# Eleven operations moved within the order of a hybrid attention/RWKV block, and one small product given to VectorE

## The chip, the cores and the metric

The kernel runs on one core of a Trainium2 chip. The metric is the device time of one execution in microseconds. A core has five instruction queues that matter here: TensorE (PE in the profile, its weight loads PEld), VectorE (DVE), ScalarE (ACT), GpSimd (POOL) and SyncE (SP), which issues the DMAs. Each engine works through its own queue strictly in order; between engines there are only semaphores.

## What is computed

The reference is one decoder block for a sequence of 512 positions and a model width of 1024: an RMS norm, one input projection, then two groups of heads side by side (native sparse attention, "NSA", and the RWKV-7 recurrence), one output projection and a gated ConvFFN. Everything is float32. Cut to what matters:

```
h = rmsnorm(x, norm1_g);  proj = h @ w_in
# attention: 8 heads, 2 groups; compressed, selected and window branch, each with its gate
o_nsa  = gates0 * softmax(q k_cmp + bias) v_cmp + gates1 * softmax(q k_sel + bias) v_sel + gates2 * softmax(q k_win + bias) v_win
# RWKV-7: 8 heads, state 64x64, 512 steps
sa = state . a
state = state * w + sa x b + v x k
y = state . r                       # then a norm over the head, + bonus, * gate g
x = x + concat(o_nsa, o_rwkv) @ w_out
h = rmsnorm(x, norm2_g);  u = causal_dwconv(h @ ffn_up)
x = x + (silu(u_gate) * u_val) @ ffn_down
```

## The kernel before

**Products.** Matrix products keep float32 accuracy by splitting each operand into a high and a low part (ACT casts `hi<-raw`, DVE or POOL subtracts `lo<-raw,hi`) and adding three products. Weights stream from DRAM through a ring of tiles.

**Stages.** `prep(j)`, j = 0 to 3, prepares two RWKV heads: the decay `sgw` (an ACT tanh, a DVE TENSOR_SCALAR, a DVE scan along time), its exponentials `W` and `iW` on ACT, the normalised key `kkn`, then `Af`, `AR`, `BK`, `BKh` (scaled copies for the chunks), `rl` (low part of the bonus product) and `Ma`, `Mr` (masked 64x64 products, from PSUM tile `rp`). `inverse(g)` inverts triangular 32x32 blocks for a pair of `prep`s: `Z <- Z,U` product and `Z <- Z` sum, 31 times. `chain(g)` then runs 16 chunk steps: in `step(c)` TensorE multiplies the state, DVE adds `UV <- rw,AV`, TensorE multiplies `UV` by `BKt`, and DVE adds `Sb <- sw,rw` (state times decay `sw <- Sb,wcs`, plus the new part); each pair of chunks gives an output `py`, normed by `norm` into `yn`. In parallel, attention has `queries` (`qd <- qs,rq`, a product by the query norm), `scores` (softmax numerators `L`, statistics `st`), `values` (`ph` cast by ACT, `pl` subtracted by DVE, then TensorE adds `ot <- ph,Vt` and `ot <- pl,Vt`) and `merge` (`of`). Output projection and ConvFFN follow, from about 370 us to the end.

**What sets the order.** The program text does not. Engines are wrapped (`_Eng`, lines 199 to 213): every call is put on a list and numbered, and `_Order.release` (line 190) issues the list at the end in the order of the table `TURNS` (line 174, 5,996 numbers, packed in the string `_TURNS`). So all instructions have line 210 in the profile and are told apart by tile names. `SWAP` (line 177) holds numbers of `tensor_tensor` calls that go to the other one of VectorE and GpSimd than their text says. Which buffer of a ring a tile takes, and so what it must wait for, follows from the same order.

```
    def release(self, turns):
        ...
            for i in turns:
                self.held[i]()
```
```
            swap = name == "tensor_tensor" and self._o.held is not None and len(self._o.held) in SWAP
            f = getattr(self._x if swap else self._e, name)
```

Of the kernel before, what the change touches and what calls it, by code (L numbers as in the profile page):

```python
# [32 lines left out]
_o = 0  # L33
for _n, _w in (("ident", 128), ("mask", 128), ("reset", 512), ("sel", 2), ("ones", 1), ("row", 1)):
# [83 lines left out]
    "j~{QtBV{oSxFCh--RAzvS~C!!K;{3P&y%0*+oJlJuk}&hw)uG(wlDm1}wpKjLeIdhwm-SI<x+m;{qNI8Keku>LVMfeFr&1jOsnAPZt}*`$oP99%Mof-izE"
    "gS33^S-GX>%)DTKkRf7Uuz|fe6u8#ng1BJkU)cRnJ`48nd>}ZXF~N2-4BO0~X@N0V7i>1${>HLkt8u&(bVE11hOV9kK^Hto_lGdgd}!vI4|x7iKj2jt^kM"
    "12!7$J8U?|V+F_di&;kW)g4}E~)!3h37!3+yV`I7NEJQx%V4m#_r+6#jMM@#t^&jWe%(6;(caE9adm3GtaS_Nf1<q*v=e+nhhJNQf=q#BBo8v1GwtIcSQo"  # L120
    "q`aVutEP|vnM6Wqo%*#EJ(-MnipBfDq405UPnqE&fg5kB$=g>)(kR<v#b34C7&<nW``q51Elxl^5llKhPD-&X_m7h73S-EI{X2~=vd8$F*;I5Yxdx}T$j6"
    "&HOLyI(RjHkgLDw@CrE;%4c<kdjvT=yfgYlfrwOtIGajSi2B-9A>LdeKggy2W?I)4*ah?5{v+Syz*3+6o8?mOd|4X#zW1Lk-aY8R>ZEDl4E;aR}e6I(kuI"
    "9i7nPrd3DcvJ`<ft6saZG<ShdFc3>0J5JY?LjsRc6U<Jtc0%SR*lJi$22@Yqe~o-uFn1uIDq3`BB(L*2;ceu4~M8%@x-AQgcHW%M#h4C&)I=m-i^o_hb{9"
    "YgXwht`S=`LL+sxE;7)mW~#qCQR20}UC26a+*av2_UMudCP=(gm&>ekg;()%Q8%(qtY5?WOMe+5qvQ?gCtK9%V+ns<tUY9moFcEAlj7(lCrA(J#`3duln&"
    "J{5|a0bgqWy~Ov##<<$QJ{w%AkNX1!%v4Bc6?C+~EX&RSEt$Ua@5D|8uku~--B%hFdvd_+FhKIHzL8uF(8nVG1p<zxn?p|;eM9$H80N=><KvKn_aS{<28R"
# [1157 lines left out]
```

## Time and profile before

| | us |
|---|---|
| three runs | 799.33, 792.83, 798.37 (median 798.37) |
| the profiled execution | 796.21, its span in the trace 794.3 |
| busy in that span: PE / DVE / ACT / POOL | 766.3 / 517.5 / 359.6 / 227.0 |
| mean granted TensorE clock | 0.984 of full |

The span is what the profiler recorded, from the first instruction to the last; 1.9 us of the profiled execution lie around it. Busy time is the time in which at least one instruction of the engine was running. In a row of the timeline, the part in square brackets is the engine's idle time just before the row and what ended it: `[1.94 <-DVE kkn L210]` is 1.94 us of idling that ended when DVE had written `kkn`.

### The profile page before, as it was taken

The page shows a single profiled execution, that of the slowest core. Times are in us where ns is not written, and L with a number is a line of the kernel's source. Part 1 is how long each engine was busy: PE and PEld are TensorE (multiplying, and loading weights), DVE is VectorE, ACT ScalarE, POOL GpSimd, SP SyncE. Part 2 cuts the span into 40 slices and gives each one's busy share as a digit, 9 for nine tenths or more (in the row PEclk, how much of TensorE's full clock was granted, in tenths as well). Part 3 has the DMA queues.
Part 4 walks back from the last instruction along what each step waited for, and adds up shares of the span by engine and source line. Part 5 has one row for each costly group of instructions (what it writes and reads, how often), then busy time and mean ns, then how long its engine had stood idle before and what let it go on. Part 6 is the DMA issues. An engine that isn't in the chain of part 4 may idle for free.

```text
span 794.3 us, 12056 instructions
## 1 busy us (share of the span) xinstructions
PE 766.3 (96%) x4152; PEld 617.0 (78%) x4152; DVE 517.5 (65%) x1078; ACT 359.6 (45%) x779; POOL 227.0 (29%) x360
## 2 busy tenths in 40 slices
...
DMA packets 59708, 67.87 MB, mean 85 GB/s; under 512 B 25710, under 2 KB 32686, under 8 KB 59648
## 3 DMA queue, kind: packets, MB, share of 16 engines
...
## 4 chain that ended last, share of the span: by engine, by line
PE 86%; DVE 7%; POOL 3%; issue 2%; ACT 1%; DMA 1%; SPq 0%; DVEq 0%; POOLq 0%; ACTq 0%
PE mm L210 31%; PE rp L210 23%; PE rw L210 21%; PE ot L210 5%; PE pre L210 4%; PE py L210 2%; POOL Z L210 1%; DVE Z L210 1%; DVE sgw L210 1%; DMA raw<-in_wst 1%; DVE Sb L210 0%; DVE sw L210 0%; DVE Ma L210 0%; DVE UV L210 0%; DVE qd L210 0%
## 5 line engine op out<-in xcount | busy, mean ns | idle before, releaser
L210 ACT CAST hi<-raw 128x512 fp32r<-128x512 f32 (+3 forms) x212 | 117.4, 584 | 127.2 <-DMA raw<-in_fdn 67.2
L210 DVE TENSOR_TENSOR lo<-raw,hi 128x512 fp32r<-128x512 f32 (+3 forms) x179 | 118.3, 672 | 39.8 <-ACT hi L210 15.4
L210 DVE SCALAR_TENSOR_TENSOR uf<-zf,fvt,uf 128x512 f32<-128x512 f32 x88 | 65.7, 749 | 29.4 <-ACT uf L210 29.4
L210 ACT ACTIVATE uf<-zf,fvt 128x512 f32<-128x512 f32 x44 | 35.8, 816 | 98.4 <-DVE zf L210 98.4
L210 POOL MEMSET zf<- 128x2 f32 x44 | 4.2, 100 | 211.3 <-DVE uf L210 107.5
L210 POOL TENSOR_TENSOR lo<-raw,hi 128x512 fp32r<-128x512 f32 (+3 forms) x33 | 39.8, 1210 | 68.3 <-ACT hi L210 28.8
L210 PE MATMUL mm<-act,hi 128*128 128x512 f32 x176 | 55.2, 395 | 0.0
L210 PE MATMUL mm<-h2h,hi 128*128 128x512 f32 x128 | 50.7, 396 | 0.0
L210 PE MATMUL mm<-h2l,hi 128*128 128x512 f32 x128 | 50.5, 395 | 0.0
L210 PE MATMUL mm<-h2h,lo 128*128 128x512 f32 x128 | 50.5, 394 | 0.0
L210 PE MATMUL rw<-h2h,hi 128*128 128x512 f32 x112 | 44.3, 395 | 0.0
L210 PE MATMUL rp<-h2l,hi 128*128 128x512 f32 x112 | 44.2, 394 | 0.0
L210 PE MATMUL rw<-h2l,hi 128*128 128x512 f32 x112 | 44.2, 394 | 0.0
L210 PE MATMUL rp<-h2h,hi 128*128 128x512 f32 x112 | 44.1, 396 | 0.0
L210 PE MATMUL rp<-h2h,lo 128*128 128x512 f32 x112 | 44.1, 394 | 0.0
L210 PE MATMUL rw<-h2h,lo 128*128 128x512 f32 x112 | 44.1, 394 | 0.0
L210 POOL TENSOR_TENSOR L<-L,st 128x512 f32<-128x512 f32 (+1 forms) x41 | 38.9, 968 | 5.7 <-PE rw L210 2.3
L210 ACT ACTIVATE L<-L,st 128x384 f32<-128x384 f32 (+3 forms) x64 | 35.4, 557 | 8.2 <-DVE st L210 5.4
L210 PEld LDWEIGHTS mm<-act,hi 128*128 128x128 f32 x176 | 33.0, 188 | 7.8
L210 PE MATMUL mm<-K,Q 128*128 128x256 f32 (+3 forms) x128 | 34.0, 362 | 2.8 <-DVE pl L210 2.1
L210 PE MATMUL mm<-act,lo 128*128 128x512 f32 x88 | 34.7, 394 | 0.0
L210 PE MATMUL mm<-XH,hi 128*128 128x512 f32 x80 | 32.8, 412 | 0.7 <-ACT hi L210 0.7
...
## 6 DMA issues: line engine op xcount, KB each, us to landing
...
```

Source lines behind the costliest of these rows:

```text
L210: self._o.held.append(lambda: f(*a, **k))
```

## The change

The packed table `_TURNS` is replaced by another of the same length, so that eleven operations stand elsewhere in the order, and one number leaves `SWAP`. A line or two of the diff:

```
-    "c-rlncbHX0(#GFDBRQubgCdHAAqR&jARuYUk|c;IK|ojmMOkuO$r(gI6v;V9k+>>?7#M<p$bbxjBbi~QtG>7UUKDkC_WAy2e$P4g+;hA8R99DbRrMJIgOU"
+    "c-rlncX(CB*2dr2k=~?*4hkyLA}wI(Ris_IpeQJUbi_+hkV|h~dXXkg6a`UwM*)MtRS`smP^3vHK`_z@$*lFgGv^?vm*+m;|K#`VefHUBX7<dQHLJ{yfkE"
...
-SWAP = {..., 2321, 2322, 2364, 2366, ...}
+SWAP = {..., 2321, 2322, 2366, ...}
```

The new file is one line shorter, so every row of it says L209. What the table moves, by place in the program (the numbers are those of the places in the text below):

1. GpSimd, the second pair of `prep`s: `XT` (a memset of a buffer that the inverse fills much later) and `AR` exchange their places around `rl`.
2. VectorE, a step of `chain(0)`: one of the two `sw <- Sb,wcs` goes up by four operations.
3. VectorE, a step later: `UV` goes ahead of `yn <- yn,py`.
4. VectorE: one `qd <- qs,rq` (128x4x64, half of a query product) goes down past `UV`, `sw`, `yb` and two `Sb`.
5. VectorE, a few steps later: `UV` goes ahead of one `Z <- Z` and of the reciprocal `zc`.
6. `st <- st,gates` (128x4) of one `scores` goes from GpSimd to VectorE, between a `CUSTOM_DVE`/accumulator read of `L` and the product `L <- L,st` that uses it.
7. VectorE, at the end of the inverse of the second pair: `pl <- rp,ph` goes ahead of the last `Z <- Z,U`, the last `Z <- Z` and a `TENSOR_SCALAR st`.
8. ScalarE, late in `chain(1)`: the first of two `yn <- py` goes behind `COPY of` and `CAST ph`.

TensorE's and SyncE's orders are the same in both.

Place 1, GpSimd's queue in the second pair of `prep`s; before:

```order
L210 TENSOR_TENSOR BKh<-BK,W 128x512
L210 MEMSET XT 128x1024
L210 TENSOR_TENSOR rl<-KR,rh 128x512
L210 TENSOR_TENSOR AR<-KR,W 128x16x32
L210 TENSOR_TENSOR lo<-raw,hi 128x512
```

and now:

```order
L209 TENSOR_TENSOR BKh<-BK,W 128x512
L209 TENSOR_TENSOR AR<-KR,W 128x16x32
L209 TENSOR_TENSOR rl<-KR,rh 128x512
L209 MEMSET XT 128x1024
L209 TENSOR_TENSOR lo<-raw,hi 128x512
```

`AR` needs the exponential `W` from ACT, `rl` and `XT` need nothing from it; `BKh` ahead of them and `lo` behind them stand where they stood.

Place 2, VectorE's queue around a step of the first chain (`z`, `VV` belong to the projection, `rq` is the query norm, `bs` a row of biases); before:

```order
L210 TENSOR_TENSOR UV<-rw,AV 32x256
L210 COPY bs<-mm 8x512
L210 SCALAR_TENSOR_TENSOR VV<-z,omm,zp 128x16x32
L210 TENSOR_TENSOR Sb<-sw,rw 64x2x64
L210 TENSOR_TENSOR yb<-yb,v_613 128x256
L210 TENSOR_TENSOR Ma<-rp,cct 128x256
L210 TENSOR_SCALAR rq<-rq 128x4x8
L210 TENSOR_TENSOR sw<-Sb,wcs 64x128
L210 TENSOR_TENSOR Sb<-sw,rw 64x2x64
```

and now:

```order
L209 TENSOR_TENSOR UV<-rw,AV 32x256
L209 COPY bs<-mm 8x512
L209 TENSOR_TENSOR sw<-Sb,wcs 64x128
L209 SCALAR_TENSOR_TENSOR VV<-z,omm,zp 128x16x32
L209 TENSOR_TENSOR Sb<-sw,rw 64x2x64
L209 TENSOR_TENSOR yb<-yb,v_613 128x256
L209 TENSOR_TENSOR Ma<-rp,cct 128x256
L209 TENSOR_SCALAR rq<-rq 128x4x8
L209 TENSOR_TENSOR Sb<-sw,rw 64x2x64
```

`sw` went from just ahead of the `Sb` that adds it to a place ahead of `VV`; behind that second `Sb` the order goes on with `Mr`, `Ma` and a `qd <- qs,rq` as before.

Places 3 and 4, VectorE's queue some three steps later (`m_629` and `yb` are the norm of `py`, `Q_582` and `Q_587` the low parts of queries); before:

```order
L210 TENSOR_TENSOR yn<-yn,py 128x256
L210 TENSOR_TENSOR UV<-rw,AV 32x256
L210 TENSOR_TENSOR sw<-Sb,wcs 64x128
L210 TENSOR_TENSOR Sb<-sw,rw 64x2x64 x2
L210 SCALAR_TENSOR_TENSOR Q_582<-rp,fvt,Q_582 64x2x256
L210 TENSOR_TENSOR qd<-qs,rq 128x4x64
L210 TENSOR_REDUCE m_629<-py 128x4
L210 TENSOR_TENSOR UV<-rw,AV 32x256
L210 TENSOR_TENSOR sw<-Sb,wcs 64x128
L210 TENSOR_SCALAR m_629<-m_629 128x4
L210 TENSOR_TENSOR yb<-py,m_629 128x256
L210 TENSOR_TENSOR Sb<-sw,rw 64x2x64 x2
```

and now:

```order
L209 TENSOR_TENSOR UV<-rw,AV 32x256
L209 TENSOR_TENSOR yn<-yn,py 128x256
L209 TENSOR_TENSOR sw<-Sb,wcs 64x128
L209 TENSOR_TENSOR Sb<-sw,rw 64x2x64 x2
L209 SCALAR_TENSOR_TENSOR Q_582<-rp,fvt,Q_582 64x2x256
L209 TENSOR_REDUCE m_629<-py 128x4
L209 TENSOR_TENSOR UV<-rw,AV 32x256
L209 TENSOR_TENSOR sw<-Sb,wcs 64x128
L209 TENSOR_SCALAR m_629<-m_629 128x4
L209 TENSOR_TENSOR yb<-py,m_629 128x256
L209 TENSOR_TENSOR Sb<-sw,rw 64x2x64 x2
L209 TENSOR_TENSOR qd<-qs,rq 128x4x64
```

`UV` and `yn` have exchanged their places at the top, and `qd` stands four operations and two `Sb` lower, ahead of `Q_587` instead of `m_629`.

## Rows read from the trace of the kernel before

**Rows 1.** Windows: stretch, length, busy time (instructions) PE, PEld, DVE, ACT, POOL, granted clock, DMA.

```profile
385.00:790.00 405.00, 405.00 (x1750) 327.21 (x1749) 225.58 (x344) 152.97 (x253) 23.82 (x60) 1.00 0.30 97
111.00:114.00 3.00, 3.00 (x15) 2.17 (x15) 2.17 (x5) 1.68 (x3) 1.23 (x1) 0.50 0.36 98
213.60:220.00 6.40, 6.38 (x27) 4.25 (x28) 5.26 (x12) 0.46 (x1) 1.85 (x3) 0.50 0.00 0
241.00:275.00 34.00, 29.01 (x258) 22.98 (x259) 30.70 (x107) 20.46 (x70) 27.84 (x61) 1.00 0.12 28
```

**Rows 2.** Timeline around place 1: start, duration (us), engine, operation, out<-in, [idle before].

```profile
103.87 1.31 DVE L210 TENSOR_SCALAR sgw<-sgw 128x512 f32<-128x512 f32 x1
...
104.87 1.46 POOL L210 TENSOR_TENSOR rl<-KR,rh 128x512 fp32r<-128x512 f32 x1
...
105.22 2.20 DVE L210 TENSOR_TENSOR_SCAN sgw<-cct,sgw 128x512 f32<-128x512 f32 x1
...
109.41 1.70 DVE L210 SCALAR_TENSOR_TENSOR Af<-kkn,W 128x512 f32<-128x512 f32 x1
...
109.53 0.30 PE L210 MATMUL rp<-cct,BKh 128*128 128x128 f32 x1 [1.94 <-DVE kkn L210]
```

**Rows 3.** Timeline of the decay of another `prep`, VectorE.

```profile
153.57 0.42 DVE L210 TENSOR_SCALAR sgw<-sgw 128x512 f32<-128x512 f32 x1
...
156.82 1.22 DVE L210 TENSOR_TENSOR_SCAN sgw<-cct,sgw 128x512 f32<-128x512 f32 x1
```

**Rows 4.** Timeline around place 2.

```profile
208.32 0.75 DVE L210 SCALAR_TENSOR_TENSOR VV<-z,omm,zp 128x512 f32<-128x512 f32 x1 [1.69 <-ACT zp L210]
...
210.42 2.73 DVE L210 TENSOR_TENSOR sw<-Sb,wcs 64x128 f32<-64x128 f32 x1
210.67 2.33 POOL L210 TENSOR_TENSOR qd<-qs,rq 128x256 f32<-128x256 f32 x4
...
213.61 0.40 POOL L210 TENSOR_TENSOR sw<-Sb,wcs 64x128 f32<-64x128 f32 x1 [0.62 <-DVE Sb L210]
213.62 0.61 PE L210 MATMUL rw<-Sb,AR 128*32 128x128 f32 x2 [3.88 <-DVE Sb L210]
...
214.09 1.06 POOL L210 TENSOR_TENSOR BKh<-BK,W 128x512 f32<-128x512 f32 x1
...
214.17 1.26 DVE L210 TENSOR_TENSOR qd<-qs,rq 128x256 f32<-128x256 f32 x1
...
215.80 0.42 DVE L210 TENSOR_TENSOR UV<-rw,AV 32x256 f32<-32x256 f32 x1
```

**Rows 5.** Timeline around places 3 and 4.

```profile
222.89 0.78 DVE L210 TENSOR_TENSOR sw<-Sb,wcs 64x128 f32<-64x128 f32 x1
...
222.91 1.22 PE L210 MATMUL rw<-UV,BKt 64*128 64x128 f32 x4 [0.65 <-DVE UV L210]
...
225.45 2.63 DVE L210 TENSOR_TENSOR qd<-qs,rq 128x256 f32<-128x256 f32 x1
...
228.91 0.37 PE L210 MATMUL rw<-UV,BKt 64*128 64x128 f32 x1 [1.23 <-DVE UV L210]
```

**Rows 6.** Timeline at places 5 (TensorE) and 6 (VectorE).

```profile
248.38 0.37 PE L210 MATMUL rw<-UV,BKt 64*128 64x128 f32 x1 [1.11 <-DVE UV L210]
...
270.96 0.85 DVE L210 TENSOR_TENSOR L<-L,st 128x512 f32<-128x512 f32 x1 [0.64 <-POOL st L210]
```

**Rows 7.** Timeline around place 7.

```profile
278.47 0.83 DVE L210 TENSOR_TENSOR Z<-Z,U 128x16 f32<-128x16 f32 x1
...
280.08 0.68 DVE L210 TENSOR_TENSOR pl<-rp,ph 128x512 fp32r<-128x512 f32 x1
...
280.81 0.50 PE L210 MATMUL mm<-K,Q 128*128 128x512 f32 x1 [2.10 <-DVE pl L210]
```

**Rows 8.** Timeline around place 8.

```profile
366.07 0.46 ACT L210 ACTIVATE yn<-py,fvt 128x128 f32<-128x128 f32 x1 [3.98 <-PE py L210]
...
367.57 0.49 PE L210 MATMUL ot<-ph,Vt 128*128 128x512 f32 x1 [1.37 <-ACT ph L210]
```

More of the change, by code (lines that the diff above doesn't have):

```diff
@@ L118 @@
[L118 to L125, printed above, removed]
@@ new lines @@
+    "krEGCP|gWH-O$(n(mw>7Ux(yX|p1#wd!#tqGg>zW67P#F10T5=N+$WPLc9LR(xNEW2$kp;zYPEV`5I_q1@2uE4cm=qxUv;cpNCf~B;X+3~icnsO_9ggc$c"
+    "nTj!MB$9q!V$ejk_k`+g>XSD<C5MW6(A~lRWsppwq1>Nk4Gfx8eGvs5jzmCm(`LVNwU_!CV%y#Uea5hZ1_dvi5p40W@pQ(@FX6_A@;f^erEeMDVYQ<1f>l"
+    "2>UqtNf-LbQ;@EOJj;|cbA(B$bildr9A}EhzdegH>f6$A%pWF`r=I$oyH>w)RCp%I+XZ0aGgd}yO#z{@Z-ejb_lQo~0Q&lYw@JSI~dXXrDoPOK|{IBUrF>"
+    ";e5xyD}qtf%y-mWsHn$Msu2?;-rk7B6z<@*?2uMIuFycoIA(J)s%8K&f2T%Q%Ve5gNr$p5HvfkYtif>fjJ1636-n)dVIuO_GqP`-AL=!v&Kz;zDrV><PXJ"
@@ new lines @@
+    "z6~<+xhLeho-*@;ok5m}uY$E4#h$>mmJlQaU;Ksb_vOnVmgil;VT}v6nBmxL{!A;3#p+;#+59&?2{swWi$Pa(#cSx|Sr~N2y>z<|^UeEaftkni`#O(To$&"
+    "@s4+(~QMg+rnZiiuPdnmv4=XuyYj0i^Z_lahBFxr<))DgkpU`WtWJ83Tr4jirJUpx=u(L>wnz~DIN?K|zN-Lxvod7=@+Ie#3b(L4B3@1;7TNG<IY#A^#`V"
+    "}~F_R;<;#Z1AK-1=RNUTLhW7S_>dMSx(JP!|O=N&-I%HStXlP*4jZ<ae7sVzZCT4-0E<oXn@R~yq<ip)=;-XE6s9Mq{9Lorz7rRtiGc;F;++E7|j)2kt=d"
+    "bas)Yo44NpHWUvnA{Uk|}jKSLo)R8+lFVH<y@(e-tV8%mK+~BC5qfD~UBE;JB)SqOo$JO>6SJ@>wrpGjmHepSt|L3XC2f3>D<FKC5XDCf)U25wQIiS0xzU"
@@ new lines @@
+    "IbSnPm^kQH_;Y*)RKe9MqF$FIUbfoh#p(b+S=5$t>BfN5xr;l@ez*>XWosD`Xwz9xHLWhR-<YXJIp0B|CMQt~6UTZ&>O}%~kzamdNLNm~7^H8OQz{AnVCo"
+    "vs{<cMr_gujnoyo*g&V5Y5wjcNz{gR5$m{lTdu1)qVp=4D2Y;2F0jr;UM0#|UB^1{-iGy;{xVWV%j?olHmZ}y68`$J_K>l1lyo;o#L-I*lOEEQ<!9??9j2"
+    "Wn)Zcv)Vv;(trfO!E@!3t-Vo!OC^*+(=yy_*rS+|pRm0h}szkkZ7RFgvZSQqOn(pN)#Kt9wr$ela2q>uiYnW&=CG6U1`j5LrQT2JarZMk7`7<V;B9a&8^s"
+    "V+5m-<_xF+d4!ynt!36<`k!?xg`rfvrA6NBPBIba`0YG>4jeCk5M{<%+z=FHGWRlMm&b;5;IMwuoa_&_&G=?kZ$^^c}oYd_5S*%w$r9)uP<^1zN8JPQ!Vu"
```

99 lines of the change are left out of this document (47 added, 52 removed).

## The prediction

> **What bounds the kernel now.** I read the windows first. From 385 us on, TensorE is busy for 405.00 of 405 us at full clock [rows 1]: output projection and ConvFFN are a solid block of matmuls, and nothing in the change touches it. So a microsecond by which TensorE starts that block earlier is a microsecond of the whole, and one that is saved anywhere and lost again before 385 us is nothing. The reader should therefore look for TensorE's idle times ahead of 385 us, in the timeline, and at what ends each. The large ones are few: 1.94 us at 109.53 [rows 2], 3.88 at 213.62 [rows 4], 0.65 and 1.23 at 222.91 and 228.91 [rows 5], 1.11 at 248.38 [rows 6], 2.10 at 280.81 [rows 7], 1.37 at 367.57 [rows 8]. Each ends with an operation of VectorE or ScalarE, and each lies at a place of the change. The windows show a second cost: after the idle times of 1.94 and 3.88 us TensorE's granted clock stands at 0.50, the lower level (1.2 GHz), while it is busy all the time: 3.00 of 3.00 us at 111 to 114, 6.38 of 6.40 at 213.6 to 220 [rows 1].
>
> **Why VectorE is late there.** Several VectorE operations take far longer than their like: a TENSOR_SCALAR 1.31 us instead of 0.42 and a scan 2.20 instead of 1.22 [rows 2, 3]; `sw` 2.73 at 210.42, where the same operation took 0.78 at 222.89, itself stretched [rows 4, 5]; `qd` 2.63 at 225.45 and 1.26 at 214.17 [rows 4, 5]. In each case GpSimd is at work, and the stretched operation ends just behind a GpSimd instruction: `sw` at 213.15, where four `qd` of GpSimd end at 213.00; `qd` at 215.43, where `BKh` ends at 215.15 [rows 4]. So VectorE is kept from memory by GpSimd, and an order that brings the two together at other times has other durations.
>
> **The change part by part.** The sum is made against the profiled execution, 796.21 us (794.3 in the span, 1.9 around it); the median of the runs is 798.37.
>
> Place 1. `AR` waits for `W`, which waits for the scan; so GpSimd now stands still while VectorE does the TENSOR_SCALAR and the scan, and `rl` and `XT` come behind. Saved ahead of `kkn`: 1.31 - 0.42 = 0.89 and 2.20 - 1.22 = 0.98, together 1.87 [rows 2, 3]; the TENSOR_SCALAR is still held by `BKh` at its start, so I take 1.8, which leaves about 0.1 of the 1.94. Behind it there are two ends. `rl` (1.46) now runs where `Af` comes, and `Af` needs both its inputs from memory: if it gets in behind `rl`, about 109, the gain is kept and the clock, which then need not fall, gives back up to 1.5 (half of the 3.00 at 0.50 [rows 1]): 3.3. If `Af` must also sit out `XT` and `lo`, it ends near 111.5 instead of 111.11 and I keep 0.9, half. Taken: **1.8**, between the two ends and with no clock gain.
>
> Place 2. `sw` now runs in the 1.69 us that VectorE spends idle ahead of `VV` [rows 4], which hides it. `Sb` then runs at 210.42, where `sw` began, and TensorE starts 2.73 us earlier. But TensorE next waits for `UV` (215.80), and ahead of it stands `qd`, which follows `sw` by 1.02 us (213.15 to 214.17), so it comes at 211.44: in the midst of GpSimd's four `qd`. Three outcomes. It sits out everything up to `BKh`: GpSimd no longer waits 0.62 us for `Sb`, so all of that is 0.62 earlier, and `UV` gains 0.6. It gets in when the four `qd` end at 213.00: it ends at 213.2 instead of 215.43, `UV` gains 2.2. It gets in at the next boundary between two of the four (0.58 us each): it ends at about 212, and `UV` gains 2.73 at least, as TensorE's start. The row nearest to it, `sw` at 210.42, sat out the same run of `qd` to its end. Taken: **1.9**, the second outcome less some weight for the first.
>
> The Trainium skill, SBUF — State Buffer, section "Who interferes with whom", says that VectorE with two SBUF inputs and GpSimd exclude each other by a lock held for one whole instruction, and that whoever issues first has it. By that rule `sw` should have waited for one `qd` of GpSimd, 0.58 us, and not for four; the trace disagrees here. Were it to hold for the `qd` of this place, the sum would hold the third outcome, which is the first rival below.
>
> Place 3. `UV` no longer stands behind a `yn` of its own size (0.42 [rows 4] and the step between): **0.45** of the 0.65 idle [rows 5]. `yn` goes to the next stage one operation later and isn't waited for there. Ends: 0 and 0.65.
>
> Place 4. The stretched `qd` leaves the way of `UV`; the 2.63 us go, and of the 1.23 us of TensorE's idling nothing is left: **1.2** [rows 5]. It now follows an `Sb` for which GpSimd waits too, so it should come first and cost its bare 0.4, ahead of `Q_587` and the next `UV`. If it doesn't, see the third rival.
>
> Place 5. `UV` goes ahead of a `Z` sum: up to 1.11 [rows 6]. But VectorE is busy for 30.70 of 34 us there [rows 1], and the order saves it no work, so most of the gain runs into the next operation that waits for VectorE. Taken: **0.4**, ends 0 and 1.1.
>
> Place 6. The small product on VectorE spares the round trip to GpSimd, 0.64 us of idling [rows 6], and costs one small operation, some 0.2: **0.4**, ends 0 and 0.6.
>
> Place 7. `pl` stood behind two `Z` operations from 278.47 to 280.08, 1.61 us [rows 7]: it can run that much earlier, and TensorE too: **1.6** of its 2.10. The `Z` operations come some 0.7 us later, except that they were waiting for GpSimd anyway (0.83 us for 16 columns); what follows them is a transfer of the inverse, with TensorE busy on attention meanwhile. Ends: 0.9, if that 0.7 is waited for, and 2.1.
>
> Place 8. ScalarE was idle for 3.98 us, waiting for the `py` of a `yn`, with `of` and `ph` behind it [rows 8]. They now go ahead in that time; TensorE's 1.37 us of waiting for `ph` goes but for a rest: **1.3**. The price, `yn` behind a cast, is at most some 0.5, and nothing on TensorE waits for it soon. Ends 0.8 and 1.37.
>
> Sum: 1.8 + 1.9 + 0.45 + 1.2 + 0.4 + 0.4 + 1.6 + 1.3 = 9.05, so 796.21 - 9.05 = 787.2, say **787**. With the low ends of all (0.9, 0.6, 0, 0.8, 0, 0, 0.9, 0.8: 4.0) it is 792; with the high ends of the single places (3.3, 2.7, 0.65, 1.2, 1.1, 0.6, 2.1, 1.37: 13.0) it is 783.
>
> **The rivals.**
>
> First, more: VectorE gets in between GpSimd's instructions, or the clock stays up behind place 2. TensorE was at 0.50 for all of 213.6 to 220 while busy [rows 1]; with the 3.88 us idle time cut, half of 6.38 us, 3.2, might come back on top. For it: `sw` at 222.89 did get in (0.78). Against it: VectorE was busy for 5.26 of these 6.40 us, so it would be the next bound. With 0.8 more at place 2, 1.5 at place 1 and 1 to 3 of the clock on the 9.05: 796.2 - 12.4 to 796.2 - 14.4, about **783**.
>
> Second, less: the gains up to place 6 are swallowed in 241 to 275, where VectorE has 30.70 and GpSimd 27.84 of 34 us [rows 1]. If VectorE's queue is what is late from there on, an earlier TensorE waits for it, and only the gains at 7 and 8 and half of those before 241 (2.7) remain: 796.2 - 5.6 = 790.6; if those before 241 go entirely, 796.2 - 2.9 = **793**. Against it: VectorE's own stretched time (0.9 + 1.0 + 2.4 + 2.2 of rows 2, 4 and 5 over their like) falls too, and TensorE's idle times are waits for particular operations, not for a queue that is always full.
>
> Third, slower: `qd` of place 4 meets GpSimd's next products and sits them out as it did before, but with `Q_587`, `UV` and TensorE behind it. The stretch would be 2.6 us again [rows 5], or about 4 with a longer run of products, and TensorE's idling for as long would pull the clock down as it did at 213.62, at a price of some 3.2 to 6 in the stretch behind. Then place 4 gives -4 - 6 instead of +1.2: the sum of 9.05 turns to about -2, and the kernel stands at **798**. It decides when `qd` is not first at the port, that is when GpSimd's `sw` starts ahead of it. The same could happen with `qd` at place 2, at a smaller price.
>
> That the change does nothing at all is excluded by the orders, since every move stands at an engine that is waited for.
>
> **How the numbers follow.** Chances: the forecast 0.45 (784 to 791), the first rival 0.2 (780 to 784), the second 0.25 (790 to 796), the third 0.1 (796 to 808). The range that leaves out some 1 in 10 on either side is 781 to 796. A measurement of this kernel tells about 1% from no change, 8 us of the median of 798.37, that is below 790.4 or above 806.4. Faster by more: most of the forecast (0.35) and the first rival (0.2), 0.55. Slower by more: the far end of the third, 0.04. Within: the rest, 0.41.
>
> **What would show it.** In the trace of the changed kernel TensorE's idle time ahead of `rp<-cct,BKh` near 109 should be under 0.4 us, with the scan at 1.2; `sw` near 206 should take 0.3, and the idle time of 3.88 should be gone or split into one of about 1 and one ahead of `UV`; `qd` behind it shows by its duration which outcome came (0.6, 1.7 or above 3); the `qd` of place 4 should take 0.4, and `pl` stand ahead of the last `Z`. The clock in the windows at 111 to 114 and 214 to 226 tells the first rival. I am wrong if any VectorE operation with two inputs from memory takes over 2 us at a new place, or if TensorE's idle times before 385 us don't fall by about 9 us in sum.

## The result, and the profile of the changed kernel

The changed kernel takes 786.38 us (median of 4 runs, 785.72 to 786.47); the kernel before took 798.18 beside it (4 runs, 792.83 to 799.33). The ratio is 0.9863, with a 95% interval from 0.9819 to 0.9908. On another chip 12 runs gave 786.39 (784.47 to 788.08), beside 29 of the kernel before with a median of 795.46 (786.69 to 799.74); the ratio there is 0.9931 [0.9899, 0.9963]. The two medians would give 0.9886; the ratio leaves out three slow runs of the kernel before, which accounts for only a part of the difference. The forecast was 787.

| | before | after |
|---|---|---|
| the profiled execution | 796.21, span 794.3 | 785.72, span 783.8 |
| busy PE / DVE / ACT / POOL | 766.3 / 517.5 / 359.6 / 227.0 | 764.1 / 512.4 / 359.6 / 225.6 |
| mean granted TensorE clock | 0.984 | 0.993 |
| TensorE's idle time between 90 and 400 us | 21.5 | 13.9 |

The windows of the changed kernel (stretch, length, busy time and instructions of PE, PEld, DVE, ACT, POOL, granted clock, DMA) answer to [rows 1]:

```profile
375.00:780.00 405.00, 405.00 (x1748) 326.95 (x1746) 225.45 (x344) 152.11 (x251) 23.17 (x59) 1.00 0.31 97
109.00:112.00 3.00, 3.00 (x25) 2.44 (x24) 3.00 (x8) 1.68 (x3) 2.99 (x3) 1.00 0.31 72
193.00:199.00 6.00, 6.00 (x26) 4.33 (x26) 5.79 (x15) 1.56 (x3) 4.88 (x2) 0.72 0.00 0
207.00:213.50 6.50, 6.24 (x46) 4.11 (x44) 5.70 (x17) 1.24 (x3) 5.33 (x10) 1.00 0.35 77
222.00:228.00 6.00, 5.89 (x19) 4.67 (x19) 2.50 (x5) 2.08 (x8) 4.22 (x7) 0.50 0.31 48
```

TensorE still has no idle time from 375 us on, so the end is moved by what happens ahead of it and by nothing else. The clock stays up at 109 to 112, behind place 1, and at 207 to 213.5, behind place 2, where it was down before [rows 1]. It is down at two new places, 193 to 199 in part and all of 222 to 228. So the total came out, but not in the way in which the sum went. A ledger shows it: how much earlier the same operation starts in the changed kernel than in the one before.

| operation | before | after | lead | what was won or lost since the row above |
|---|---|---|---|---|
| scan of an earlier `prep` | 87.60 | 87.20 | 0.40 | ahead of every move |
| `UV` | 187.46 | 184.80 | 2.66 | place 1: +2.3 |
| `UV` | 205.08 | 203.84 | 1.24 | with the clock at half from 194.5 to 198: -1.4 |
| `UV` | 215.80 | 209.36 | 6.44 | place 2: +5.2 |
| `UV` | 222.43 | 212.92 | 9.51 | the clock that stayed up, and place 3: +3.1 |
| `UV` | 228.45 | 216.07 | 12.38 | place 4: +2.9 |
| `Lt` | 235.13 | 228.64 | 6.49 | a new stall at `sw`, and the clock behind it: -5.9 |
| `UV` | 255.40 | 248.56 | 6.84 | place 5: +0.3 |
| `pl` | 269.19 | 262.56 | 6.63 | -0.2, no place of the change |
| `pl` | 272.77 | 265.98 | 6.79 | place 6: +0.2 |
| `pl` | 290.63 | 281.49 | 9.14 | place 7: +2.4 |
| `pl` | 363.52 | 354.35 | 9.17 | nothing |
| `pl` | 375.09 | 364.34 | 10.75 | place 8: +1.6 |

The span ends 10.5 us earlier. Between 188 and 229 us the kernel was 12 us ahead, as the first rival had it, and half of this was lost again within ten microseconds.

Not all of the ledger is the work of the moves. The two traces took different courses ahead of place 2, at an operation of GpSimd that no move touches:

```profile
201.97 4.04 POOL L210 TENSOR_TENSOR rq<-rq,mhalf 128x12 f32<-128x12 f32 x1
```

in the kernel before, and in the changed one:

```profile
199.30 2.27 POOL L209 TENSOR_TENSOR rq<-rq,mhalf 128x12 f32<-128x12 f32 x1
```

In the traces of this kernel, of the changed one and of their variants below, it takes either 4.04 or 2.27 us. Wherever it takes 2.27, TensorE's clock was at half for a part of the stretch from 193 to 201 us, and the step from the `UV` of the ledger's second row to the next took 19.0 us; wherever it takes 4.04, the clock stood at 1.00 there and this step took 17.6. The order up to this operation does not decide: runs of the changed kernel with edits that come later took either course. What does decide is not shown, and one trace of a run cannot tell how often each comes. So the -1.4 and a part of the +5.2 of place 2 belong to the course (see place 2 at the end).

**Place 1** in the timeline of the changed kernel (start, duration, engine, operation, [idle before]), against [rows 2]:

```profile
103.46 0.42 DVE L209 TENSOR_SCALAR sgw<-sgw 128x512 f32<-128x512 f32 x1
103.92 1.23 DVE L209 TENSOR_TENSOR_SCAN sgw<-cct,sgw 128x512 f32<-128x512 f32 x1
...
107.15 1.73 DVE L209 SCALAR_TENSOR_TENSOR Af<-kkn,W 128x512 f32<-128x512 f32 x1
...
114.05 0.38 PE L209 MATMUL rp<-AR,BK 64*128 64x128 f32 x2 [0.84 <-DVE BK L209]
```

The TENSOR_SCALAR takes 0.42 and the scan 1.23 us; TensorE's 1.94 us of idling are gone. `Af` is stretched as it was before (1.73, before 1.70), so it sat out `rl` and nothing more. A new idle time of 0.84 us comes later, and one of 0.38 us at 117.26.

**Place 2**, against [rows 4]:

```profile
205.43 0.29 DVE L209 TENSOR_TENSOR sw<-Sb,wcs 64x128 f32<-64x128 f32 x1
...
207.53 2.52 POOL L209 TENSOR_TENSOR qd<-qs,rq 128x256 f32<-128x256 f32 x4 [0.24 <-DVE rq L209]
...
208.48 0.52 DVE L209 TENSOR_TENSOR qd<-qs,rq 128x256 f32<-128x256 f32 x1
...
209.36 0.42 DVE L209 TENSOR_TENSOR UV<-rw,AV 32x256 f32<-32x256 f32 x1
```

`sw` at 205.43 takes 0.29 us. The `qd` behind it, the one with three outcomes, is let in among GpSimd's four and takes 0.52; `UV` follows 0.88 us after its start. The idle time of 3.88 us is gone, and with it the half clock behind it. `VV`, which waited 1.69 us for `zp` in the kernel before, does not wait here: that is the other course.

**Places 3 and 4**, against [rows 5]:

```profile
213.40 0.71 PE L209 MATMUL rw<-UV,BKt 64*128 64x128 f32 x4 [0.26 <-DVE UV L209]
...
216.30 0.40 POOL L209 TENSOR_TENSOR sw<-Sb,wcs 64x128 f32<-64x128 f32 x1
...
216.52 3.06 DVE L209 TENSOR_TENSOR sw<-Sb,wcs 64x128 f32<-64x128 f32 x1
...
218.81 0.61 POOL L209 TENSOR_TENSOR qd<-qs,rq 128x256 f32<-128x256 f32 x1
...
220.75 0.42 DVE L209 TENSOR_TENSOR qd<-qs,rq 128x256 f32<-128x256 f32 x1
...
220.87 0.30 PE L209 MATMUL rp<-cct,kdup 128*128 128x128 f32 x1 [2.05 <-DVE Sb L209]
```

TensorE's wait at place 3 is 0.26 us (before 0.65). Then comes what the sum had not: at 216.52 another `sw`, which nobody moved, takes 3.06 us: it ends at 219.58, just behind the row of GpSimd's products, which ends at 219.42. TensorE idles for 2.05 us, and its clock is at 0.50 from 222 to 228. `qd` of place 4 stands behind this, at 220.75, and takes its bare 0.42.

**Places 5 to 8**, VectorE's and TensorE's lines at 6 to 8, against [rows 6], [rows 7] and [rows 8]:

```profile
263.61 0.55 DVE L209 TENSOR_TENSOR st<-st,gates 128x4 f32<-128x4 f32 x1
...
272.38 0.74 PE L209 MATMUL mm<-K,Q 128*128 128x512 f32 x2 [0.42 <-DVE pl L209]
...
273.63 0.74 PE L209 MATMUL mm<-K,Q 128*128 128x512 f32 x2 [0.45 <-DVE st L209]
...
356.10 0.48 PE L209 MATMUL ot<-ph,Vt 128*128 128x512 f32 x1
```

`UV` of place 5, at 240.07, now waits for TensorE (0.18), not the other way. `st` of place 6 takes 0.55 on VectorE, more than the 0.2 that I gave it. At place 7 TensorE's wait for `pl` is 0.42 instead of 2.10; one of 0.45 follows at 273.63. At place 8 the product `ot <- ph,Vt` has no idle time ahead of it, and `yn` comes behind, at 356.89.

### The profile page after: what moved, and what is told of

The parts are those of the page before. It is cut to its first block, busy times and chain, and to the rows that moved or that the text cites. A ratio compares the mean times of both kernels' runs of the same rounds, so it can differ in the third digit from the quotient of the medians.

```text
span 783.8 us, 12054 instructions
## 1 busy us (share of the span) xinstructions
PE 764.1 (97%) x4152; PEld 615.5 (79%) x4152; DVE 512.4 (65%) x1079; ACT 359.6 (46%) x779; POOL 225.6 (29%) x359
## 4 chain that ended last, share of the span: by engine, by line
PE 86%; DVE 7%; POOL 3%; DMA 1%; issue 1%; ACT 1%; SPq 0%; DVEq 0%; POOLq 0%
PE mm L209 31%; PE rp L209 23%; PE rw L209 21%; PE ot L209 5%; PE pre L209 4%; PE py L209 2%; POOL Z L209 2%; DVE Z L209 1%; DMA raw<-in_wst 1%; DVE sw L209 1%; DVE kkn L209 0%; DVE UV L209 0%; DVE sgw L209 0%; DMA raw<-in_wtC 0%; DVE Sb L209 0%
## 5 line engine op out<-in xcount | busy, mean ns | idle before, releaser
L209 ACT CAST hi<-raw 128x512 fp32r<-128x512 f32 (+3 forms) x212 | 117.3, 584 | 124.9 <-DMA raw<-in_fdn 67.6
L209 DVE TENSOR_TENSOR lo<-raw,hi 128x512 fp32r<-128x512 f32 (+3 forms) x179 | 117.5, 667 | 38.5 <-ACT hi L209 14.3
L209 DVE SCALAR_TENSOR_TENSOR uf<-zf,fvt,uf 128x512 f32<-128x512 f32 x88 | 65.7, 750 | 29.1 <-ACT uf L209 29.1
L209 ACT ACTIVATE uf<-zf,fvt 128x512 f32<-128x512 f32 x44 | 35.8, 816 | 98.5 <-DVE zf L209 98.5
L209 POOL MEMSET zf<- 128x2 f32 x44 | 4.2, 100 | 211.3 <-DVE uf L209 107.1
L209 POOL TENSOR_TENSOR lo<-raw,hi 128x512 fp32r<-128x512 f32 (+3 forms) x33 | 40.1, 1220 | 67.9 <-ACT hi L209 25.6
L209 PE MATMUL mm<-act,hi 128*128 128x512 f32 x176 | 55.3, 395 | 0.0
L209 PE MATMUL mm<-h2h,hi 128*128 128x512 f32 x128 | 50.7, 396 | 0.0
L209 PE MATMUL mm<-h2l,hi 128*128 128x512 f32 x128 | 50.6, 395 | 0.0
L209 PE MATMUL mm<-h2h,lo 128*128 128x512 f32 x128 | 50.5, 394 | 0.0
L209 PE MATMUL rw<-h2h,hi 128*128 128x512 f32 x112 | 44.3, 395 | 0.0
L209 PE MATMUL rp<-h2l,hi 128*128 128x512 f32 x112 | 44.2, 395 | 0.0
L209 PE MATMUL rw<-h2l,hi 128*128 128x512 f32 x112 | 44.2, 395 | 0.0
L209 PE MATMUL rp<-h2h,lo 128*128 128x512 f32 x112 | 44.2, 395 | 0.0
L209 PE MATMUL rw<-h2h,lo 128*128 128x512 f32 x112 | 44.2, 394 | 0.0
L209 PE MATMUL rp<-h2h,hi 128*128 128x512 f32 x112 | 44.1, 395 | 0.0
L209 POOL TENSOR_TENSOR L<-L,st 128x512 f32<-128x512 f32 (+1 forms) x41 | 38.9, 966 | 5.1 <-PE rw L209 2.3
L209 ACT ACTIVATE L<-L,st 128x384 f32<-128x384 f32 (+3 forms) x64 | 35.5, 557 | 8.7 <-DVE st L209 8.7
L209 PEld LDWEIGHTS mm<-act,hi 128*128 128x128 f32 x176 | 33.1, 188 | 7.8
L209 PE MATMUL mm<-K,Q 128*128 128x256 f32 (+3 forms) x128 | 34.0, 360 | 1.7 <-DVE st L209 0.8
L209 PE MATMUL mm<-act,lo 128*128 128x512 f32 x88 | 34.8, 396 | 0.0
L209 PE MATMUL mm<-XH,hi 128*128 128x512 f32 x80 | 33.1, 416 | 0.7 <-ACT hi L209 0.7
```

The lines of the kernel that those rows point to most:

```text
L209: self._o.held.append(lambda: f(*a, **k))
```

## The experiments

Two theories stood at the start. A: each place gives what the ledger shows, and the stalls at `sw` and `qd` come from a meeting with GpSimd at one port, which the order decides. B: the places do little by themselves; moving one only shifts the stall to the next operation. In the diffs a number in `TURNS` is one operation; `(x, y)` in the loop puts `x` right behind `y`, and the loop itself is left out after the first diff. A number in `SWAP` has its engine exchanged; the text gives `sw` to GpSimd, in two halves, one for partitions 0 to 63 and one for 64 to 127.

**Place 2 undone in the changed kernel.** 1827 is the `sw` that was moved; it goes back.

```diff
+for x, y in ((1827, 1588),):
+    TURNS.remove(x)
+    TURNS.insert(TURNS.index(y) + 1, x)
```

> The changed kernel with place 2 alone undone: sw stands again just ahead of its Sb. Theory A (each place's gain is its own, and in the changed kernel the stretch of places 2 to 4 gained 3.8 us net): sw meets GpSimd's four qd again, TensorE idles for about 3.9 us near 211 and its clock is at 0.50 behind it; places 3 and 4 still give 0.45 and 1.2, so the time is about 2.2 us above the changed kernel's, 788.6. Theory B (place 2 only handed the stall on to the sw that took 3.06 us at 216.52 in the changed kernel, and to the fall of the clock behind it): undoing it changes nothing beyond 1 us, 785.4 to 787.4, and the sw of 216.52 takes less than 1 us.

Measured: 789.07 us (10 runs), 0.9944 [0.9906, 0.9983] of the kernel before (795.00 on that chip); the changed kernel has 786.39 elsewhere. Its timeline around the place, and at the other `sw`:

```profile
209.59 2.73 DVE L212 TENSOR_TENSOR sw<-Sb,wcs 64x128 f32<-64x128 f32 x1
...
212.79 0.60 PE L212 MATMUL rw<-Sb,AR 128*32 128x128 f32 x2 [3.89 <-DVE Sb L212]
...
225.08 2.04 DVE L212 TENSOR_TENSOR sw<-Sb,wcs 64x128 f32<-64x128 f32 x1
...
228.42 0.41 PE L212 MATMUL rp<-cct,kdup 128*128 128x128 f32 x2 [1.58 <-DVE Sb L212]
```

The stall and the idle time of [rows 4] are back, 2.73 and 3.89 us. But the time grows by less than the 8.3 us that the ledger has for place 2, its clock and place 3: by 1.0 us if the ratio 0.9944 is held against 0.9931, by 6.4 against 0.9863, and the intervals overlap, so it is not known more closely than some 1 to 6 us. One reason stands in the trace: the `sw` at 225.08 is stalled for 2.04 us here instead of 3.06, and TensorE waits 1.58 us instead of 2.05. Part of what place 2 wins is lost at the next meeting; in that B is right.

**Place 2 alone in the kernel before.**

```diff
+for x, y in ((1827, 1828),):
```

> The kernel before with place 2 alone done. Theory A: TensorE starts 2.7 us earlier there, its clock stays up, and the 6.4 us at 0.50 shrink by up to 3: the idle time of 3.88 us is gone, the time is 3 to 6 us below the kernel before, about 793.5. Theory B: the next VectorE product with two inputs from memory (qd ahead of UV, 2.63 us in the kernel before) is held the longer, and the time is within 1.5 us of the kernel before.

Measured: 792.03 us (10 runs), 0.9997 [0.9957, 1.0038]. The time doesn't tell it from the kernel before.

```profile
211.43 0.53 DVE L213 TENSOR_TENSOR qd<-qs,rq 128x256 f32<-128x256 f32 x1
...
219.21 0.39 POOL L213 TENSOR_TENSOR sw<-Sb,wcs 64x128 f32<-64x128 f32 x1
...
219.52 3.10 DVE L213 TENSOR_TENSOR qd<-qs,rq 128x256 f32<-128x256 f32 x1
...
223.44 0.37 PE L213 MATMUL rw<-UV,BKt 64*128 64x128 f32 x1 [2.80 <-DVE UV L213]
```

The idle time of 3.88 us is gone and `qd` takes 0.53, as in the changed kernel. This trace too has the course with 2.27 us for `rq`, so not all of that need be the move's. At 219.52 the other `qd`, that of place 4, takes 3.10 us just behind a `sw` of GpSimd, and TensorE waits 2.80 us. The kernel before has this stall too, with 2.63 and 1.23 us [rows 5]; it has grown. So in its place the move does what was expected, and in the net B is right: alone it gains nothing that can be measured, and the larger stall at `qd` is one that place 4 takes away in the changed kernel.

**Place 1 alone in the kernel before.** `rl` goes behind `AR`, and the memset of `XT` behind `rl`.

```diff
+for x, y in ((350, 724), (832, 350)):
```

> The kernel before with place 1 alone done (AR ahead of rl and XT on GpSimd). Theory A: 2.2 us less than the kernel before, about 796, since the changed kernel's trace stood 2.25 us better behind this place, with TensorE's idle time of 1.94 us gone, one of about 0.8 us ahead of rp<-AR,BK in its stead, and no fall of the clock at 111 to 114. Theory B: what is gained there is lost again in VectorE's and GpSimd's full stretch from 241 to 275, so the time is within 1 us of the kernel before.

Measured: 794.09 us (10 runs), 1.0005 [0.9954, 1.0056]: 2.2 us are 0.28% and lie within the interval.

```profile
105.22 1.22 DVE L213 TENSOR_TENSOR_SCAN sgw<-cct,sgw 128x512 f32<-128x512 f32 x1
```

The scan takes its 1.22 us, and the idle times left near there are of 0.64 us at 115.35 and 0.37 at 118.56. The gain at the place is there; that it reaches the end is not shown by this run.

**The stalled `sw` given to GpSimd**, in the changed kernel: 1890 is the half for partitions 64 to 127 that VectorE computes.

```diff
+SWAP -= {1890}
```

> The changed kernel, with the sw that took 3.06 us at 216.52 on VectorE given back to GpSimd, where it queues among the products that held it up. Theory A (that stall and the fall of the clock behind it cost the changed kernel some 5.9 us of a gain of 12.4): TensorE's idle time of 2.05 us at 220.87 goes, the clock does not fall at 222 to 229, and the time is 3 to 5 us below the changed kernel, about 782.5. Theory B (the stall only goes to the next VectorE product with two inputs from memory, the qd of place 4): qd takes 2 us or more and the time is within 1 us of the changed kernel, 785.4 to 787.4.

Measured: 784.16 us (10 runs), 0.9889 [0.9843, 0.9935]. The stall at `sw` is gone. But `qd` behind place 2 has one in this trace:

```profile
206.51 0.39 POOL L210 TENSOR_TENSOR sw<-Sb,wcs 64x128 f32<-64x128 f32 x1
...
206.87 2.33 POOL L210 TENSOR_TENSOR qd<-qs,rq 128x256 f32<-128x256 f32 x4
...
207.61 1.87 DVE L210 TENSOR_TENSOR qd<-qs,rq 128x256 f32<-128x256 f32 x1
```

It takes 1.87 us and ends just behind the last of GpSimd's four `qd`, which followed a `sw` of GpSimd without a gap. In the changed kernel GpSimd had idled for 0.24 us between the two (the row at 207.53 above). The edit cannot have put this stall there: the order is the changed kernel's up to the edited `sw`, which comes at 219.46. It goes with the course: `rq` takes 4.04 us here, `VV` waits 1.35 us for `zp`, and GpSimd comes to its `qd` without the pause. From `UV` at 201.29 to `UV` at 209.84 it is 8.55 us, against 10.72 in the kernel before, which has the same course, and 5.52 in the changed kernel's own trace. The time lies between what A and B gave.

**The meeting by itself.** A program of 40 blocks that computes nothing of the reference: GpSimd runs four to six products on 128 partitions without a gap, and VectorE comes in with one target (`sw`, `qd` or a TENSOR_SCALAR of those shapes) after a preamble of 0 to 7 operations that read PSUM.

```
        for m in range(8):
            block([qd] * 6, sw, m)      # and qd, TENSOR_SCALAR; trains of kdup; a mixed train
```

> Not the block but the disputed cost by itself: 40 short blocks, in each of which GpSimd runs a train of products (six qd-like 128x256, four kdup-like 128x512, or qd, qd, kdup, qd) and VectorE, let go by the same ScalarE copy, does 0 to 7 products 128x64 from PSUM and then one target with inputs from SBUF: a sw-like 64x128 product, a qd-like 128x256 product, or a TENSOR_SCALAR 128x512. Nothing of the reference is computed. Theory A (one GpSimd instruction holds it up at most, and the next boundary lets it in): no target takes longer than its bare time (0.28, 0.4, 0.4 us) plus one GpSimd instruction (0.6 us of a qd, 1.05 of a kdup). Theory B (it sits out the whole train): the duration falls with the number of products ahead, from about 3.5 us at the start of a train of six qd to its bare time behind it. Theory C (it depends on the moment at which it comes): at some offsets bare or one instruction more, at others to the end of the train, for the same pair of operations.

Four targets began before the train did. The other 36 were all let in when the GpSimd instruction that was running had ended, and finished 0.15 to 0.3 us behind that; none took over 1.09 us. One block (lines of its own program; `run` is GpSimd's, `tsw` the target):

```profile
12.95 2.37 POOL L1178 TENSOR_TENSOR run<-st,go 128x256 f32<-128x256 f32 x4 [1.06 <-ACT go L1194]
13.11 0.59 DVE L1186 TENSOR_TENSOR tsw<-st,go 64x128 f32<-64x128 f32 x1
```

The target begins in the midst of a train of four and is through in 0.59 us. That is what the Trainium skill says (SBUF — State Buffer, section "Who interferes with whom": a lock for one whole instruction, whoever issues first). So a row of products is not enough to keep VectorE out for 3 us. In the block something else belongs to it.

**The changed kernel again**, on this other chip, no edit.

> The changed kernel once more, on the chip of the runs beside it. Its four runs first shown lay within 0.1%, those of kernels close to it spread by 1%. If the operations of places 2 to 4 are let in or held up by chance, its time spreads like theirs, 781 to 790, and its trace shows another of VectorE's products held up for 2 us or more between 205 and 225, or none; if the order fixes it, it is sw at 216.5 again with 3 us, and the runs lie within 0.3%.

Measured: 786.39 us, as above. `sw` at 215.32 took 3.05 us again, and TensorE idled 2.05 us. This stall came in both traces of the changed kernel, so the order fixes it as far as two traces can show; the 12 runs lie within 3.6 us, 0.46%, wider than the 0.3% that was expected of a fixed order and narrower than the 781 to 790 of chance. Both have the course with 2.27 us for `rq`.

**All four products to GpSimd**: both halves of the two `sw` near place 4, and the two `qd` that VectorE computes.

```diff
+for x, y in ((1873, 1872), (1890, 1889)):
+SWAP -= {2288, 1873, 1890, 1735}
```

> The changed kernel, with VectorE's four products of two inputs from memory between 205 and 225 (two sw, two halves of qd) given back to GpSimd, each sw just behind its other half. Theory A (what the stretch loses is VectorE being held up): no VectorE operation there is stretched over 1 us, TensorE's idle times between 200 and 225 sum to under 1.5 us, the clock does not fall behind them, the time is 3 to 5 us below the changed kernel, 782, and it spreads less. Theory B (GpSimd becomes the late one, with 0.4 to 0.6 us more for each): TensorE waits for Sb behind GpSimd's sw, as long in sum as in the changed kernel, and the time is within 1 us of it.

Measured: 786.90 us (12 runs), 0.9908 [0.9874, 0.9943], no better than the changed kernel.

```profile
216.86 0.87 POOL L213 TENSOR_TENSOR sw<-Sb,wcs 64x128 f32<-64x128 f32 x2
...
218.11 0.73 PE L213 MATMUL rw<-Sb,AR 128*32 128x128 f32 x4 [2.52 <-DVE Sb L213]
```

VectorE is never kept out, but GpSimd is late: `Sb` waits 2.95 us for its two `sw`, and TensorE 2.52 us for `Sb`. B is right here.

**The `sw` of the stall to GpSimd, and early**, right behind its other half.

```diff
+for x, y in ((1890, 1889),):
+SWAP -= {1890}
```

> As e4, but the sw given to GpSimd also stands just behind its other half, ahead of a qd. Theory A: 0.6 us less than e4 at most, 3 to 5 below the changed kernel beside it. Theory B (the stall goes to another VectorE product): within 1 us of the changed kernel, with qd behind place 2 or qd of place 4 at 1.8 us or more.

Measured: 786.66 us (12 runs), 0.9924 [0.9892, 0.9956]. The time is what B gave. `sw` is gone from VectorE, and `Sb` waits 1.60 us for GpSimd's two halves instead. The `qd` behind place 2, at 211.21, took 1.87 us again, and the clock was at 0.50 from 214 to 224; but that comes ahead of the edited operation (222.03) and is the course of e4_sw624_gpsimd again, with 4.04 us for `rq` and 8.58 us from `UV` to `UV`. So it is no stall that the edit has moved there.

**Which GpSimd instruction keeps VectorE out.** In every trace so far a stall over more than one GpSimd instruction came behind a `sw` of GpSimd on partitions 0 to 63 with products following it without a gap: at 216.30 in the changed kernel, at 206.51 in e4_sw624_gpsimd, at 219.21 in e2_only_sw610, and in the kernel before at

```profile
210.31 0.39 POOL L210 TENSOR_TENSOR sw<-Sb,wcs 64x128 f32<-64x128 f32 x1
...
224.68 0.39 POOL L210 TENSOR_TENSOR sw<-Sb,wcs 64x128 f32<-64x128 f32 x1
```

just ahead of the stalled operations at 210.42 and 225.45 [rows 4, 5]. So trains were headed by a product on 128x128, on partitions 0 to 63, or on 64 to 127, in 32 blocks again without anything of the reference.

```
        low, upp, full = part(slice(0, 64)), part(slice(64, 128)), part(slice(0, 128))
        for first in (low, upp, full):
            for m in (0, 2, 4, 6):
                block([first] + [qd] * 5, sw, m)
```

> The disputed cost by itself once more, nothing of the reference computed. In every trace so far VectorE's product sat out more than one GpSimd instruction only where GpSimd's unbroken train began with, or had just done, a product sw on 64 of the 128 partitions; in e5 all trains had 128 partitions and all 40 targets were let in at the next boundary. Trains now begin with a 64-partition product (lower or upper half), or, as the control, with one of the same size on 128 partitions, followed by five qd; some have it in the middle or ahead of two kdup. Theory A (a 64-partition product ahead in the train shuts VectorE out until GpSimd's train ends): targets in trains with the half end 0.15 to 0.3 us behind the train's end, taking up to 3 us, and those in the control, or ahead of the half in the middle, end 0.15 to 0.3 behind the next boundary, under 0.9 us. Theory B (the half has nothing to do with it): all targets under 0.9 us in all trains, and what shut VectorE out in the block is something that these trains lack.

Three blocks: headed by the lower half, by the upper half, and by 128 partitions (`run` at L1187 is the head, at L1178 the products, `tsw` the target):

```profile
8.32 0.39 POOL L1187 TENSOR_TENSOR run<-st,go 64x128 f32<-64x128 f32 x1 [1.27 <-ACT go L1200]
8.59 3.12 DVE L1187 TENSOR_TENSOR tsw<-st,go 64x128 f32<-64x128 f32 x1
8.68 2.88 POOL L1178 TENSOR_TENSOR run<-st,go 128x256 f32<-128x256 f32 x5
...
45.01 0.40 POOL L1187 TENSOR_TENSOR run<-st,go 64x128 f32<-64x128 f32 x1 [1.06 <-ACT go L1200]
45.28 0.29 DVE L1187 TENSOR_TENSOR tsw<-st,go 64x128 f32<-64x128 f32 x1
...
85.31 0.40 POOL L1187 TENSOR_TENSOR run<-st,go 128x128 f32<-128x128 f32 x1 [1.06 <-ACT go L1200]
...
85.85 0.58 DVE L1187 TENSOR_TENSOR tsw<-st,go 64x128 f32<-64x128 f32 x1
```

Behind the lower half the target waits for the whole train: it ends at 11.71, 0.15 us after the fifth product. Behind the upper half it takes 0.29, behind 128 partitions 0.58. It was so without an exception: 15 of 15 targets that came behind a lower half in an unbroken train sat it out to the end (1.68 to 3.49 us; `sw`, `qd` and TENSOR_SCALAR targets, trains of `qd` and of `kdup`, the half at the head or in the middle), and of the 17 others 14 came behind a head (7 an upper half, 7 on 128 partitions) and were let in at the next boundary, in 0.81 us at most; three began ahead of their head or half. So A holds, with one limit: it is the lower half, and not any half. Behind an upper half GpSimd's next product began 0.07 to 0.08 us after the end of the head, while behind the other two heads it began 0.03 to 0.04 us before it. For the upper half these blocks don't tell the partitions from that small gap; the heads on 128 partitions, which have no gap and let the target in, show that a train without a gap is not enough. Why the chip does it isn't shown.

**The halves exchanged in the changed kernel.** If that is the cause, GpSimd should compute the upper half where products follow. In one `sw` the halves change their turns on GpSimd (1863 is the lower, 1864 the upper); in the stalled one they change engines, the lower (1889) now on VectorE.

```diff
+for x, y in ((1864, 1831), (1863, 1713), (1890, 1877), (1889, 1888)):
+SWAP -= {1890}
+SWAP |= {1889}
```

> The changed kernel, with the halves of two sw exchanged between the engines or in the order: where GpSimd did the lower 64 partitions of sw at the head of a train of qd and VectorE the upper 64, GpSimd now does the upper and VectorE (or a later place on GpSimd) the lower. Work and operations are the same. Theory A (in e9 only the lower half shut VectorE out, in 15 of 15 trains): sw that took 3.06 us and qd behind place 2 take under 0.9 us each, TensorE's idle times between 200 and 225 sum to under 1.2 us, the clock does not fall behind them, and the time is 3 to 5 us below the changed kernel, 782. Theory B (the halves are no matter in the block, or the upper half, which is written 0.3 us later, makes GpSimd late by as much): sw or qd takes over 1.5 us again and the time is within 1.5 us of the changed kernel, 785 to 788.

Measured: 782.75 us (6 runs, 782.32 to 786.12), 0.9872 [0.9830, 0.9915] of the kernel before beside it (794.91). It has the lowest median of all, with the same amount of work on each engine. But its interval overlaps those of the changed kernel, which was not run on this chip, so the time does not show it to be faster; the durations show that the stalls are gone.

```profile
210.07 0.38 PE L214 MATMUL rw<-Sb,AR 128*32 128x128 f32 x2 [1.13 <-DVE Sb L214]
...
210.62 0.82 DVE L214 TENSOR_TENSOR qd<-qs,rq 128x256 f32<-128x256 f32 x1
...
221.76 0.27 DVE L214 TENSOR_TENSOR sw<-Sb,wcs 64x128 f32<-64x128 f32 x1
```

`sw` takes 0.27 us instead of 3.06, and both `qd` take 0.82 and 0.84 us (at 223.53) with GpSimd's products beside them. The fair comparison for the `qd` behind place 2 is the run with the same course (`rq` 4.04 us) and the same order up to there but for the halves: 1.87 us in e4_sw624_gpsimd. Two parts of A did not come: TensorE's idle times between 200 and 225 sum to 2.0 us and not under 1.2, and the clock was still down to 0.56 between 210 and 216. The largest of them, 1.13 us, comes behind a `VV` that waits 1.37 us for `zp`, as in e4_sw624_gpsimd (1.13 and 1.35), so it is not of this kind.

**The same exchange in the kernel before**, with none of the eleven moves.

> The kernel before, its order untouched but for the same exchange of halves of two sw. Theory A: the two stalls that places 2 and 4 were to cure are of this kind, so sw (2.73 us) and the qd ahead of UV (2.63) take under 1 us without being moved, TensorE's idle time of 3.88 us shrinks under 1.5 and that of 1.23 to under 0.5, and the time is 3 to 6 us below the kernel before, about 791. Theory B: both are stretched as before, and the time is within 1.5 us of the kernel before.

Measured: 786.65 us (12 runs), 0.9917 [0.9882, 0.9952], the time of the whole change.

```profile
210.17 0.29 DVE L215 TENSOR_TENSOR sw<-Sb,wcs 64x128 f32<-64x128 f32 x1
210.93 0.40 POOL L215 TENSOR_TENSOR sw<-Sb,wcs 64x128 f32<-64x128 f32 x1 [1.97 <-DVE Sb L215]
...
217.78 0.71 PE L215 MATMUL rw<-UV,BKt 64*128 64x128 f32 x4 [1.33 <-DVE UV L215]
...
219.86 0.49 DVE L215 TENSOR_TENSOR qd<-qs,rq 128x256 f32<-128x256 f32 x1
...
221.18 0.71 PE L215 MATMUL rw<-UV,BKt 64*128 64x128 f32 x4 [0.20 <-DVE UV L215]
```

`qd` of place 4, unmoved, takes 0.49 us where it took 2.63 in the kernel before and 3.10 in e2_only_sw610, which has this trace's course: what place 4 cures by moving an operation out of a meeting, the exchange cures where it stands. `sw` of place 2, unmoved, takes 0.29 us where it took 2.73, but this does not test the halves. The upper half needs an `Sb` that comes behind this `sw`, so GpSimd waits for it (1.97 us) and its train starts only when `sw` is through. TensorE's wait at place 4 is 0.20 us instead of 1.23. Its largest between 205 and 225 us is that of place 3, 1.33 instead of 0.65, where the unmoved `yn` waits 1.08 us for GpSimd ahead of `UV`; its clock was 1.00 throughout. The trace has the course with 2.27 us for `rq`.

## Why the prediction was right, and where it was not

**The bound** was read rightly. TensorE is solid from 375 us on, its idle time from 90 to 400 us fell by 7.7 us (21.52 to 13.85), and the span by 10.5. The rest, 2.8, I put to the clock: TensorE's busy time fell by 2.2 with the same work. It was not quite so that each large idle time lies at a place of the change: three of 0.78 to 0.86 us (at 269.17, 273.50 and 287.40 in the kernel before) have no move, and in the changed kernel they are there again with 0.77 to 0.86.

**Place 1** was right in its mechanism: taken 1.8, measured 2.3. `Af` sat out `rl` alone and the clock at 109 to 112 stayed at 1.00, as in the upper of the two ends; that it isn't 3.3 fits the new idle time of 0.84 us. The run of this place alone was too coarse to show it in the time.

**Place 2.** I weighed three outcomes for `qd` by the row nearest to it, the `sw` that sat out four products, and took 1.9. In the changed kernel's trace the third came: let in at the next boundary, 0.52 us, and `UV` 5.2 us earlier, with 3.1 more by the clock and place 3. But that trace has another course than the one in which the rows were read. In the two runs with the order of the changed kernel up to there and the course of the kernel before (e4_sw624_gpsimd and e8_sw624_early), the second outcome came: `qd` sat out the four, 1.87 us, `UV` was 2.1 to 2.2 us earlier (8.55 and 8.58 us instead of 10.72), and the clock was at 0.50 behind it all the same (210 to 214 and 214 to 224). So for its own course the term was right, and what the prediction left out is that the course ahead of the place can be another. About 3 us of the 5.2 go with the course; whether the change had a part in it is not shown.

What the prediction held against the Trainium skill's rule was an exception with a cause: that `sw` came behind a GpSimd product on partitions 0 to 63 in an unbroken train, as `qd` does in the runs with the second outcome, and where the third came GpSimd had paused for 0.24 us. The trace of before had what was needed to suspect it (the lower `sw` at 210.31 ahead of the stall at 210.42, the one at 224.68 ahead of that at 225.45, and `qd` at 214.17 let in behind a single `BKh`), but the partitions of a 64x128 operation stand in the program and not in a row of the profile, and I did not look there.

**Place 3** can't be told from the clock in the ledger; TensorE's wait fell by 0.39 (0.65 to 0.26), taken 0.45. **Place 4** was right for `qd` itself (0.42), with `UV` 2.9 us earlier, and TensorE's product behind it 2.2 (213.40 to 217.19 against 222.91 to 228.91), where I took 1.2 from TensorE's idle time; but I gave nothing to what would be late next. The third rival said that an operation would sit out GpSimd's products there, at 2.6 to 4 us, and pull the clock down, at 3.2 to 6 more. That came, at 5.9 us for both, at the unmoved `sw` beside `qd` instead of at `qd`. It was a row of the order that I had shown: `sw` right behind `UV`, both of which places 2 and 3 pull forward into GpSimd's products.

**The sum of places 2 to 4** was then 11.1 - 5.9 = 5.2 us, less 1.4 for the clock near 194.5 to 198: 3.8 against 3.55 predicted. An error of +7.6 and two of -5.9 and -1.4 nearly cancelled. In this trace the first rival was true up to 216 us and the third, in another place, behind it; 787 as a total owes something to luck. The first rival's price for the clock was read too small: the windows [rows 1] end at 220 us, but in the kernel before the clock stood at 0.50 from 213.6 to 226, with TensorE busy for 11.74 of 12.40 us.

Of the two signs of being wrong that the prediction named, one came: the `sw` at 216.52, a product of two inputs from memory, unmoved but at a new time, took 3.06 us. The other nearly did: the idle time fell by 7.7 us, not by about 9.

**Place 5**: taken 0.4, measured 0.3. **Place 6**: taken 0.4, measured 0.2 at most; `st` took 0.55 and not 0.2, and TensorE's wait ended little earlier. **Place 7**: taken 1.6, measured 2.4. The idle time fell by 1.68 (2.10 to 0.42), and one of 0.45 came new. The rest is a term that I had at nothing, the clock, for I had seen it fall only behind the idle times of 1.94 and 3.88 us. In the kernel before it was at half behind the 2.10 us too, with TensorE busy all the time (window 281.60 to 284.80), and in the changed kernel it is 1.00 from 272 to 276:

```profile
281.60:284.80 3.20, 3.20 (x11) 2.65 (x11) 2.11 (x7) 0.00 (x0) 1.84 (x2) 0.50 0.49 75
```

Half of the 3.20 us, 1.6, is my estimate of the most that this gives back; 1.68 less 0.45 leaves 1.2 of the 2.4 for it.

**Place 8**: taken 1.3, measured 1.6.

**The second rival** (gains swallowed in 241 to 275) did not come: the lead was 6.5 us ahead of that stretch and 6.8 behind it.

**The chances.** The time lies where the forecast had 0.45 (784 to 791). By the ratio on the first chip, 0.9863, the kernel is faster by over 1%, which had 0.55; by that on the second, 0.9931, it is within 1%, which had 0.41, and that interval only just reaches the line. The range of 781 to 796 held it.
